# Convolution by half tiles on through the retention, and block 2's output products in another order

## The chip, the cores and the metric
The kernel runs on one core of a Trainium2 chip. The metric is the device time of one execution in microseconds (us); smaller is better. The kernel before took 3770.49 us, the median of three runs (3765.96 to 3771.38). One other execution, the profiled one, took 3763.95 us, of which the trace spans 3762.0.

Engines by the names of the trace: PE multiplies matrices (PEld loads its weights), DVE, ACT and POOL work on elements, SP issues most transfers. A tile has 128 partitions; "128x512" is 128 partitions by 512 elements. PSUM is the memory that PE writes into, in banks of 128x512 f32; SBUF holds everything else on the chip.

## The reference
Three blocks of a network follow one another on 1024 tokens of width 1024. The first is attention, a gated feed-forward layer and a gate. The third is a state-space layer (S5) with a second one behind it. The change is in the second:

```
proj = u @ w_in                       # conv a, b, gate; q, k, v, gate of the retention
a = conv_a * sigmoid(conv_b)
a = causal depthwise conv(a, 31 taps) # each channel by itself, along the tokens
a = silu(layernorm(a))                # over the 1024 channels
y_conv = (a @ conv_pw) * silu(conv_gate)
q, k = rotary(q), rotary(k)
r = retention(q, k, v)                # 4 heads, chunks of 128 tokens, a state from chunk to chunk
y_ret = groupnorm(r) * silu(ret_gate)
y = concat(y_conv, y_ret) @ w_out     # rows 0..1023 of w_out for y_conv, 1024..2047 for y_ret
h = rmsnorm(h + gate * y)
```

## The kernel before, in words
Activations lie with channels on the partitions: 8 tiles of 128 channels x 1024 tokens. A product in full precision (`mm3`, L225 on) splits both operands in a high and a low part (`split`: ACT copies the high part, L159; DVE or POOL subtracts it, L160) and runs three matmuls for each 128 rows and each 512 tokens: high x high (L234), high x low (L235), low x high (L236). One column block of an output is 8 x 3 x 2 = 48 matmuls of 128x512; `weights` loads its 512 KB through a ring of three SBUF tiles called `raw`, which other loads and stores of 128x1024 share.

Block 2 runs in stages. Their order in each engine's queue is fixed when the program is built.
- *Products of w_in with the convolution* (trace 1600 to 2115 us). Products of conv, gate, q, k and v are made by a scheme with seven smaller products (L638 to L640, added up in L650 to L659); 18 groups of 84 matmuls fall into 1690 to 2095. Beside them DVE does the 31 x 8 = 248 taps of the convolution as background jobs (L1149, L1153), each on 128x1024, with the sum in a PSUM tile of two banks. Background jobs stand in a list; products pay into a counter (`rate`, RQ = 6 beside q and k, RT = 8 otherwise), and whenever it holds one, one job is put into the program. What is left is drained before the retention.
- *Retention* (2115 to 2340): 16 steps of 256 tokens (4 heads x 4), each with a mask product (L1369), a state update (L1395, L1397), products out (L1385, L1388), and a normalisation (L1409 to L1415). PE's gaps are filled with the products of the convolution's gate (`fill`). The LayerNorm of the convolution is background work here, RB = 13: sums over channels (POOL, L1268), mean (PE and ACT, L1274, L1275), centring (DVE, L1279), squares (ACT, POOL), scaling (DVE, L1299) and silu. Each head's output is turned (PE, L1426), gated (L1431, L1433) and stored to `yret` (L1435). `X` is then split from the convolution's tiles `A`.
- *Pointwise layer and output products, first half* (2340 to 2546). First `conv_pw` on X (evacuated in L1460 times the gate, split into `G`), then w_out's rows 0 to 1023 on G, evacuated in L1474 onto `hr` (h scaled in the same loop) and stored to `h2`; beside them the loads of `yret` and their split into X, and tables for the S5 block as background work (L1559 and others).
- *block2_out* (2546 to 2640): w_out's rows 1024 to 2047 on X, added to `h2`.

PSUM for products: three banks `mm` and a two-bank tile `acc`, lent anew at some places by `banks()`; two `pa`, two `pb`, one `pc`.

Of the kernel before, what the change touches and what calls it, by code (L numbers as in the profile page):

```python
# [32 lines left out]
RQ = 6  # L33
RT = 8
# [3 lines left out]
RB = 13  # L38
# [19 lines left out]
class Core:  # L58


    def __init__(self, ctx, tc, ins):
# [12 lines left out]

        self.lent = ctx.enter_context(ExitStack())
        self.banks()
# [1056 lines left out]
def block2(core, X, scratch, tabs, keep, after):  # L1133
# [7 lines left out]
    with ExitStack() as st:  # L1141
        cvp = st.enter_context(tc.tile_pool(name="b2_conv", bufs=1, reuse_waits="tile"))
        A = [cvp.tile([P, PAD + S], F32, tag=f"a{c}", name=f"cv_{c}") for c in range(KT)]

        def tap(c, j, state):
# [13 lines left out]
        core.banks("psum_conv")  # L1159
        with tc.tile_pool(name="b2_mix", bufs=1, reuse_waits="tile") as pool:  # L1160
# [37 lines left out]
            def conv(_, c, a, b):  # L1198
# [4 lines left out]
                core.bg += [tap(c, j, state) for j in range(CW)]  # L1203
# [52 lines left out]
            core.paced = None  # L1256
            core.drain()
        scratch["mixed"].close()
        core.banks()
        with tc.tile_pool(name="b2_ret", bufs=1, reuse_waits="tile") as pool:  # L1260
            ln = {}

            def ln_sum(c):
                if c == 0:
                    return
                if c == 1:
                    ln["acc"] = pool.tile([P, S], F32, tag="lnacc", name="ln_acc")
                nc.gpsimd.tensor_tensor(ln["acc"], A[0][:, PAD:] if c == 1 else ln["acc"], A[c][:, PAD:], ALU.add)  # L1268

            def ln_mean():  # L1270
                ln["mu"] = pool.tile([P, S], F32, tag="lnmu", name="ln_mu")
# [5 lines left out]
            def ln_center(c):  # L1277
                a = A[c][:, PAD:]
                nc.vector.tensor_tensor(a, a, ln["mu"], ALU.subtract)  # L1279
                if c == 0:  # L1280
                    ln["var"] = pool.tile([P, S], F32, tag="lnacc", name="ln_var")
                    nc.scalar.activation(ln["var"], a, AF.Square)
                else:
                    sq = core.raw()
                    nc.scalar.activation(sq, a, AF.Square)
                    nc.gpsimd.tensor_tensor(ln["var"], ln["var"], sq, ALU.add)

            def ln_rstd():
                ln["r"] = core.rsqrt(core.token_sums(ln["var"], pool), pool)

            def ln_rows():
                ln["r"] = core.rows(ln["r"], pool)

            def ln_spread():
                ln["rb"] = core.over_partitions(ln["r"], pool, tag="lnmu")
# [10 lines left out]
            def ln_ready(c):  # L1306
                ln_sum(c)

# [3 lines left out]
            core.bg += pause * 4 + [ln_mean] + pause * 4 + [lambda c=c: ln_center(c) for c in range(KT)]  # L1312
            core.bg += pause * 8 + [ln_rstd] + pause * 2 + [ln_rows] + pause * 2 + [ln_spread] + [lambda c=c: ln_scale(c) for c in range(KT)]
# [7 lines left out]
            def conv_gates():  # L1321
                nxt = core.weights(w_in, 0, KT, 2 * D)
                for c in range(KT):
                    w = nxt
                    for half in range(2):
                        ps = core.psum("mm")
                        for k in range(KT):
# [1293 lines left out]
```

## Time and profile before

| | before |
|---|---|
| median of three runs | 3770.49 us (3765.96 to 3771.38) |
| profiled execution / its span | 3763.95 us / 3762.0 us |
| granted clock of PE, mean | 0.957 |
| PE busy | 3450.0 us, 92% of the span |
| DVE busy | 2562.5 us, 68% |
| POOL busy | 1801.3 us, 48% |
| ACT busy | 1568.7 us, 42% |
| chain that ended last: PE / DVE / POOL / DMA | 58% / 13% / 11% / 8% |

Busy shares are means over the whole span; a stage may have another limit, so the rows below are cut by stage. [...] A wait "A <- B" is idle time of A's engine that ended when B was done.

### The profile page before, as it was taken

To read this page: it belongs to the slowest core of one execution; us is meant where nothing else is said; L and a number is where in the kernel's file an instruction comes from. 1 tells how busy PE (TensorE), PEld (TensorE's weight loads), DVE (VectorE), ACT (ScalarE), POOL (GpSimd) and SP (SyncE) were. 2 spreads that over 40 slices of the span, in tenths; PEclk is the share of its full clock that TensorE was granted. 3 is DMA by queue.
4 is the path that set the end of the run, shared out by engine and by line. 5 is a ranking of instruction groups with operands and counts; after the bars stand their busy time and mean duration, and the time that the engine had idled before them with its cause. 6 is when DMAs were issued, how large, how long until landed. Compare 5 with 4: busy or idle time off the path is not lost.

```text
span 3762.0 us, 45800 instructions
## 1 busy us (share of the span) xinstructions
PE 3450.0 (92%) x16540; PEld 2777.5 (74%) x16540; DVE 2562.5 (68%) x3211; ACT 1568.7 (42%) x2729; POOL 1801.3 (48%) x1690
## 2 busy tenths in 40 slices
PE   8999999899998999798889999899899689799998
PEld 7878777777776778576667778678677478577776
DVE  7888897777767556768989665874566366655644
ACT  5666674433334444532223343125443124753334
POOL 2343343456554534477777542427338873331122
PEclk9999999999999999899989999999899899799999
DMA  4111026333325323322212444465443134325513
GB/s 142 37 32 35 28 71 233 107 96 107 107 93 185 112 76 122 113 68 79 79 56 89 139 151 128 116 215 175 135 142 101 52 109 127 96 84 188 176 47 110
DMA packets 431134, 409.84 MB, mean 109 GB/s; under 512 B 34060, under 2 KB 364348, under 8 KB 430908
## 3 DMA queue, kind: packets, MB, share of 16 engines
q1 hardware_dynamic: 396164, 330.27, 28.6%
q0 software_dynamic: 21088, 68.19, 5.0%
q10 hardware_dynamic: 13655, 8.46, 0.8%
q8 instruction: 131, 2.15, 0.2%
q14 instruction: 96, 0.78, 0.1%
HBM read 284.80 MB, written 122.03 MB: 108 GB/s over the span
## 4 chain that ended last, share of the span: by engine, by line
PE 58%; DVE 13%; POOL 11%; DMA 8%; issue 6%; ACT 4%; SPq 0%; ACTq 0%; POOLq 0%; DVEq 0%
PE mm L234 9%; PE mm L236 9%; PE mm L235 9%; PE pb L640 4%; PE pb L638 4%; PE pb L639 4%; DVE wlo L160 3%; PE pa L638 3%; PE pa L640 3%; PE pa L639 3%; POOL sc L1863 2%; POOL s_H L1865 2%; POOL s_H L1864 2%; POOL wlo L160 2%; ACT whi L159 1%
## 5 line engine op out<-in xcount | busy, mean ns | idle before, releaser
L159 ACT ACTIVATE whi<-raw 128x512 fp32r<-128x512 f32 (+3 forms) x610 | 430.9, 736 | 791.2 <-PE pb L639 216.8
L160 DVE TENSOR_TENSOR wlo<-raw,whi 128x512 fp32r<-128x512 f32 (+3 forms) x456 | 551.2, 1231 | 218.4 <-ACT whi L159 214.8
L234 PE MATMUL mm<-x,whi 128*128 128x512 f32 x1152 | 463.1, 403 | 9.3 <-ACT whi L159 4.4
L236 PE MATMUL mm<-x,wlo 128*128 128x512 f32 x1152 | 458.7, 399 | 6.0 <-DVE wlo L160 6.0
L235 PE MATMUL mm<-x,whi 128*128 128x512 f32 x1152 | 461.6, 401 | 0.5 <-DVE x L163 0.3
L493 POOL TENSOR_TENSOR s<-s,f 128x127 f32<-128x127 f32 (+1 forms) x192 | 193.8, 1017 | 294.1 <-DVE f L492 187.5
L1153 DVE SCALAR_TENSOR_TENSOR acc<-cv,par,acc 128x1024 f32<-128x1024 f32 x232 | 298.1, 1285 | 4.3
L638 PE MATMUL pa<-x,whi 128*128 128x512 f32 x648 | 261.5, 404 | 22.5 <-ACT u L659 15.1
L234 PE MATMUL mm<-yc,whi 128*128 128x512 f32 (+1 forms) x656 | 267.4, 408 | 9.2 <-ACT whi L159 5.8
L235 PE MATMUL mm<-yc,whi 128*128 128x512 f32 (+1 forms) x656 | 265.6, 405 | 6.0 <-DVE yc L160 5.9
L640 PE MATMUL pa<-x,wlo 128*128 128x512 f32 x648 | 260.0, 402 | 11.3 <-DVE wlo L160 11.1
L639 PE MATMUL pa<-x,whi 128*128 128x512 f32 x648 | 259.4, 400 | 7.5 <-DVE x L160 7.5
L236 PE MATMUL mm<-yc,wlo 128*128 128x512 f32 (+1 forms) x656 | 263.7, 403 | 1.7 <-DVE wlo L160 1.5
L640 PE MATMUL pb<-x,wlo 128*128 128x512 f32 x576 | 233.3, 410 | 31.2 <-POOL wlo L160 22.5
L234 PEld LDWEIGHTS mm<-x,whi 128*128 128x128 f32 x1152 | 220.2, 191 | 56.2 <-ACT whi L159 4.9
L638 PE MATMUL pb<-x,whi 128*128 128x512 f32 x576 | 236.6, 411 | 26.3 <-ACT whi L159 8.8
L236 PEld LDWEIGHTS mm<-x,wlo 128*128 128x128 f32 x1152 | 219.7, 191 | 52.6 <-DVE wlo L160 7.1
L160 POOL TENSOR_TENSOR wlo<-raw,whi 128x512 fp32r<-128x512 f32 x154 | 215.9, 1421 | 80.6 <-ACT whi L159 80.5
L235 PEld LDWEIGHTS mm<-x,whi 128*128 128x128 f32 x1152 | 220.2, 191 | 45.6 <-DVE x L163 0.6
L639 PE MATMUL pb<-x,whi 128*128 128x512 f32 x576 | 233.2, 405 | 3.1 <-DVE x L160 3.1
L492 DVE TENSOR_TENSOR_SCAN f<-f 128x128 f32<-128x128 f32 (+1 forms) x192 | 195.8, 1034 | 39.5 <-ACT f L485 38.3
L607 POOL TENSOR_TENSOR raw<-raw 128x512 f32<-128x512 f32 x58 | 80.0, 1379 | 246.8 <-DMA raw<-in_ffn_w_in_dram 120.9
(600 smaller groups left out, 8437.0 us busy)
## 6 DMA issues: line engine op xcount, KB each, us to landing
raw<-in_w_in_dram SPq DMA_DIRECT2D x96, 512.0 KB
raw<-in_ffn_w_in_dram SPq DMA_DIRECT2D x44, 512.0 KB
raw<-in_w_out_dram SPq DMA_DIRECT2D x32, 512.0 KB
g<-g_dram SPq DMA_DIRECT2D x56, 256.0 KB
raw<-in_sb_w_in_dram SPq DMA_DIRECT2D x24, 512.0 KB
raw<-in_ada_w_dram SPq DMA_DIRECT2D x24, 512.0 KB
raw<-h_dram SPq DMA_DIRECT2D x18, 512.0 KB
g_dram<-t POOLq DMA_DIRECT2D x8, 1024.0 KB, 4.7
```

Of the source, the lines that this page charges most:

```text
L159: nc.scalar.activation(hi, src, AF.Copy)
L160: return (eng or nc.vector).tensor_tensor(lo, src, hi.bitcast(F32), ALU.subtract).ins
L234: nc.tensor.matmul(ps, w_h, x[:, 0, sl], start=start and k == 0, stop=False)
L235: nc.tensor.matmul(ps, w_h, x[:, 1, sl], start=False, stop=False)
L236: self.last = nc.tensor.matmul(ps, w_l, x[:, 0, sl], start=False, stop=stop and k == n - 1).ins
L492: nc.vector.tensor_tensor_scan(rev, rev, rev, 1.0, ALU.mult, ALU.bypass)
L493: nc.gpsimd.tensor_tensor(s[:, :m - 1], s[:, :m - 1], f[:, 1:m], ALU.mult)
L607: self.eng.tensor_tensor(at["s1"], at["a21"], at["a22"], ALU.add)
L638: nc.tensor.matmul(ps, hi[:, i], x[i][:, 0], start=first and i == 0, stop=False, skip_group_check=more)
L639: nc.tensor.matmul(ps, hi[:, i], x[i][:, 1], start=False, stop=False, skip_group_check=more)
L640: self.core.last = nc.tensor.matmul(ps, lo[:, i], x[i][:, 0], start=False, stop=i == self.N - 1, skip_group_check=more).ins
L1153: nc.vector.scalar_tensor_tensor(out, A[c][:, j:j + S], core.vec("conv_w_2", j * KT + c), state["acc"], ALU.mult, ALU.add)
```

## The change
- The convolution's taps are on half tiles, 128x512, 496 of them, second half of the tokens first; their sum lies in one PSUM bank, `cv`. They are no longer drained before the retention but run on through it.
- PSUM for products: `mm` has two banks in the whole program (three before); `cv` one.
- The LayerNorm's sums and mean stay behind the taps; its centring, variance, scaling and a new split of the convolution into its own tiles `conv` run beside the output products, RY = 7. The S5 tables follow as the last of these jobs, at RS = 2.5 from the last two column blocks on.
- After the retention, `yret` is loaded and split into X, then w_out's rows 1024 to 2047 run first, evacuated onto hr and stored to `h2`. Then the pointwise layer runs on `conv` and is split into X. block2_out does w_out's rows 0 to 1023.
- RQ 9 (6), RT 11 (8), RB 15 (13). The last column of the convolution's gate takes its two halves by turns.

```diff
@@ -30,12 +30,14 @@
 
 
 SB = 6
-RQ = 6
-RT = 8
+RQ = 9
+RT = 11
+RY = 7
+RS = 2.5
 NS = 2
 VA = 0
 VB = 4
-RB = 13
+RB = 15
 PC = 1
 ZR = 10
 YM = 5
-    def banks(self, name="psum_mm"):
-
-        self.lent.close()
-        self.psm = self.lent.enter_context(self.tc.tile_pool(name=name, bufs=1, space=PSUM))
-
     def psum(self, tag, shape=(P, HALF)):
-        pool, bufs = {"mm": (self.psm, 3), "acc": (self.psm, 1), "pa": (self.ps, 2), "pb": (self.ps, 2), "pc": (self.ps, 1)}[tag]
-        return pool.tile(list(shape), F32, tag=tag, name=self.nm(tag), bufs=bufs)
+        bufs = {"mm": 2, "cv": 1, "pa": 2, "pb": 2, "pc": 1}[tag]
+        return self.ps.tile(list(shape), F32, tag=tag, name=self.nm(tag), bufs=bufs)
...
+                at = PAD - CW + 1 + j + half * HALF
                 if j == 0:
-                    state["acc"] = core.psum("acc", (P, S))
-                    nc.vector.tensor_scalar(state["acc"], A[c][:, :S], core.vec("conv_w_2", c),
+                    state["acc"] = core.psum("cv")
+                    nc.vector.tensor_scalar(state["acc"], A[c][:, at:at + HALF], core.vec("conv_w_2", c),
                                             core.vec("conv_b_2", c), ALU.mult, ALU.add)
                     return
-                out = A[c][:, PAD:] if j == CW - 1 else state["acc"]
-                nc.vector.scalar_tensor_tensor(out, A[c][:, j:j + S], core.vec("conv_w_2", j * KT + c), state["acc"],
-                                               ALU.mult, ALU.add)
+                out = A[c][:, PAD + half * HALF:PAD + (half + 1) * HALF] if j == CW - 1 else state["acc"]
+                nc.vector.scalar_tensor_tensor(out, A[c][:, at:at + HALF], core.vec("conv_w_2", j * KT + c),
+                                               state["acc"], ALU.mult, ALU.add)
             return run
-        core.banks("psum_conv")
...
-                core.bg += [tap(c, j, state) for j in range(CW)]
+
+                core.bg += [tap(c, j, half, state) for half in (1, 0) for j in range(CW)]
                 core.bg += [lambda: ready.append(c)]
...
-            core.paced = None
-            core.drain()
...
+            def ln_split(c):
+                if c == KT - 1:
+                    lns.close()
+                pool = parts.enter_context(tc.tile_pool(name=f"b2_c{c}", bufs=1, side="right", reuse_waits="tile"))
+                t = conv[c] = pool.tile([P, 2, S], R32, tag="c", name=f"cv_x{c}")
+                core.split(t[:, 0], t[:, 1], A[c][:, PAD:])
+                cvs[c].close()
+
+            def tables():
+                tabs["pool"] = parts.enter_context(tc.tile_pool(name="s5_tab", bufs=1, side="right", reuse_waits="tile"))
+                core.bg += s5_tables(core, tabs)
+
...
-            core.bg += pause * 4 + [ln_mean] + pause * 4 + [lambda c=c: ln_center(c) for c in range(KT)]
-            core.bg += pause * 8 + [ln_rstd] + pause * 2 + [ln_rows] + pause * 2 + [ln_spread] + [lambda c=c: ln_scale(c) for c in range(KT)]
+            core.bg += pause * 2 + [ln_mean]
+            lnjobs += [lambda c=c: ln_center(c) for c in range(KT)]
+            lnjobs += pause * 2 + [ln_rstd] + pause * 2 + [ln_rows] + pause * 2 + [ln_spread]
+            lnjobs += [lambda c=c: ln_scale(c) for c in range(KT)] + [lambda c=c: ln_split(c) for c in range(KT)[::-1]]
+            lnjobs += [tables]
...
-        for half in range(2):
-            for c in range(KT):
-                core.split(X[c][:, 0, hs(half)], X[c][:, 1, hs(half)], A[c][:, PAD + half * HALF:PAD + (half + 1) * HALF])
+        parts = st.enter_context(ExitStack())
+        rp = parts.enter_context(tc.tile_pool(name="b2_r1", bufs=1, side="right", reuse_waits="tile"))
+        wts = core.weights(w_out, D, KT, 0)
+        for c in range(KT):
+            raw = core.raw()
+            nc.sync.dma_start(raw, yret[c])
+            core.split(X[c][:, 0, :], X[c][:, 1, :], raw)
+        r1b = core.over_partitions(core.rows(scratch["r1"], rp), rp, tag="r1b")
+        core.bg += lnjobs
+        core.rate = RY
+        for m in range(KT):
+            if m:
+                wts = core.weights(w_out, D, KT, m * P)
+            if m == KT - 2:
+                core.rate = RS
+            hr = core.raw()
+            nc.sync.dma_start(hr, scratch["h"][m])
+            nc.vector.scalar_tensor_tensor(hr, hr, core.vec("final_norm", m), r1b, ALU.mult, ALU.mult)
+            ps = [core.psum("mm") for half in range(2)]
+            if m == 0:
+                for k in range(KT):
+                    for half in range(2):
+                        core.mm3(ps[half], wts, X[k:k + 1], half, k0=k, start=k == 0, stop=k == KT - 1)
+            for half in range(2):
+                if m:
+                    core.mm3(ps[half], wts, X, half)
+                nc.vector.scalar_tensor_tensor(hr[:, hs(half)], ps[half], core.mod[:, 2 * KT + m:2 * KT + m + 1],
+                                               hr[:, hs(half)], ALU.mult, ALU.add)
+            nc.gpsimd.dma_start(scratch["h2"][m], hr)
+        for m in range(KT):
+            wts = core.weights(w_pw, 0, KT, m * P)
+            sg = core.raw()
+            nc.sync.dma_start(sg, sgate[m])
+            for half in range(2):
+                ps = core.psum("mm")
+                core.mm3(ps, wts, [conv[c] for c in range(KT)], half)
+                nc.vector.tensor_tensor(sg[:, hs(half)], ps, sg[:, hs(half)], ALU.mult)
+                core.split(X[m][:, 0, hs(half)], X[m][:, 1, hs(half)], sg[:, hs(half)])
+        core.drain()
+        core.rate = 0
...
-            core.bg += s5_tables(core, tabs)
-            core.rate = 1.5
-            for m in range(KT):
...
-            wts = core.weights(w_out, D, KT, m * P)
+            wts = core.weights(w_out, 0, KT, m * P)
```

On DVE, at the end of the retention: `rtk` is the retention's output being normalised, `rs` its reciprocal deviation, `raw` of L1460 a gated pointwise result. Before:

```order
L1410 BN_AGGR mv_3141_18315<-bs_3142_18316 128x2
L1410 BN_AGGR mv_3141_18315<-bs_3143_18319 128x2
L1412 TENSOR_SCALAR rs_3144_18322<-mv_3141_18315 128x2
L1415 TENSOR_SCALAR rtk_3140_18307<-rtk_3140_18307,mv_3141_18315,rs_3144_18322 128x256 x2
L1460 TENSOR_TENSOR raw_3169_18572<-mm_3170_18574,raw_3169_18572 128x512
L1460 TENSOR_TENSOR raw_3169_18572<-mm_3175_18615,raw_3169_18572 128x512
L271 CAST rrow_3157_18468<-b2_r1_12895 128x8
L1684 MEMSET s5_pw_18779 128x32
```

and after (here L1150 is a tap, L154 a split of a loaded yret tile, L1273 a centring):

```order
L1421 TENSOR_SCALAR rs_3136_18470<-mv_3133_18463 128x2
L1150 SCALAR_TENSOR_TENSOR cv_3131_18448<-cv_7_13237,par_79,cv_3131_18448 128x512 x3
L1424 TENSOR_SCALAR rtk_3132_18453<-rtk_3132_18453,mv_3133_18463,rs_3136_18470 128x256 x2
L1150 SCALAR_TENSOR_TENSOR cv_3131_18448<-cv_7_13237,par_79,cv_3131_18448 128x512 x12
L154 TENSOR_TENSOR x_6_6583<-raw_3157_18633,x_6_6583 128x1024
L1150 SCALAR_TENSOR_TENSOR cv_3131_18448<-cv_7_13237,par_79,cv_3131_18448 128x512
L154 TENSOR_TENSOR x_7_6584<-raw_3158_18637,x_7_6584 128x1024
L1150 SCALAR_TENSOR_TENSOR cv_3131_18448<-cv_7_13237,par_79,cv_3131_18448 128x512 x11
L1150 SCALAR_TENSOR_TENSOR cv_7_13237<-cv_7_13237,par_79,cv_3131_18448 128x512
L1273 TENSOR_TENSOR cv_0_13209<-cv_0_13209,ln_mu_16959 128x1024
L1273 TENSOR_TENSOR cv_1_13213<-cv_1_13213,ln_mu_16959 128x1024
```

Of the convolution 25 half taps of the last channel and the splits of `x_6` and `x_7` stand behind the last normalisation (the shown row of L1150 x3 is ahead of it), and seven more centrings follow the rows shown before the first L1467 (scaling of h) and L1476 (evacuation of an output product); before, evacuations of the pointwise layer and first S5 tables stood there.

On PE, at the same place: L1426 (after: L1435) turns the last head's output, `pb` its bank. Before:

```order
L234 MATMUL mm_3175_18615<-x_3_6583,whi_3167_18568 128x512
L235 MATMUL mm_3175_18615<-x_3_6583,whi_3167_18568 128x512
L236 MATMUL mm_3175_18615<-x_3_6583,wlo_3168_18569 128x512
L1426 MATMUL pb_3148_18347<-ident_74,rtk_3140_18307 128x128
L234 MATMUL mm_3175_18615<-x_4_6584,whi_3167_18568 128x512
L1426 MATMUL pb_3148_18347<-ident_74,rtk_3140_18307 128x128 x3
L235 MATMUL mm_3175_18615<-x_4_6584,whi_3167_18568 128x512
L236 MATMUL mm_3175_18615<-x_4_6584,wlo_3168_18569 128x512
L234 MATMUL mm_3175_18615<-x_5_6585,whi_3167_18568 128x512
```

and after (L228 to L230 are the matmuls of a product, L1268 the mean of the LayerNorm, L277 a row spread over the partitions; `mm_3164` and `mm_3165` are the two halves of the first column block, `mm_3176` of the second):

```order
L228 MATMUL mm_3165_18669<-x_7_6584,whi_3149_18605 128x512
L229 MATMUL mm_3164_18668<-x_7_6584,whi_3149_18605 128x512
L230 MATMUL mm_3164_18668<-x_7_6584,wlo_3150_18606 128x512
L229 MATMUL mm_3165_18669<-x_7_6584,whi_3149_18605 128x512
L230 MATMUL mm_3165_18669<-x_7_6584,wlo_3150_18606 128x512
L1268 MATMUL pc_3146_18593<-ln_acc_16958,onesm_16960 128x512
L1268 MATMUL pc_3147_18596<-ln_acc_16958,onesm_16960 128x512
L277 MATMUL pc_3161_18645<-ident_71,rrow_3159_18641 128x128 x8
L277 MATMUL pc_3162_18655<-ident_71,rrow_3159_18641 128x128 x8
L228 MATMUL mm_3176_18756<-x_0_6577,whi_3173_18749 128x512
```

Before, the turning stands within a pointwise product. After, the turning (just ahead of these rows) is followed by the 12 matmuls of `x_6` and `x_7`, the last two of the eight row blocks of the first column block, of which the shown ones are the end; the other six stood between the retention's steps. Then come the mean and the spread rows, and then the second column block.

On SP, the loads there (`yret` tiles, `h`, weights of w_out); before, `yret` loads came one or two with each column block:

```order
L1362 DMA gate_3101_18307<-gate_dram_107 128x2x256
L1455 DMA raw_3157_18633<-yret_dram_92 128x1024
L1455 DMA raw_3158_18637<-yret_dram_92 128x1024
L1466 DMA raw_3163_18665<-h_dram_90 128x1024
L210 DMA raw_3172_18747<-in_w_out_2_dram 128x8x128
L1466 DMA raw_3175_18753<-h_dram_90 128x1024
L210 DMA raw_3183_18829<-in_w_out_2_dram 128x8x128
```

The load of `raw_3172`, the second column block's weights, now stands behind the loads of all eight `yret` tiles; its staging tile is the one that the first block's `h2` store empties.

## Rows read from the trace of the kernel before

**Rows 1.** Windows by stage: start:end, us, busy time (instructions) of PE, PEld, DVE, ACT, POOL, clock, DMA share, GB/s.
```profile
1651.00:1690.00 39.00, 39.00 (x171) 31.89 (x170) 37.70 (x34) 13.38 (x23) 30.62 (x23) 1.00 0.19 54
1690.00:2095.00 405.00, 357.79 (x1468) 279.83 (x1467) 363.75 (x323) 117.23 (x207) 300.09 (x216) 0.94 0.24 75
2115.00:2210.00 95.00, 84.58 (x408) 69.87 (x406) 56.01 (x82) 32.61 (x48) 56.23 (x43) 0.93 0.53 167
2210.00:2340.00 130.00, 130.00 (x672) 111.94 (x672) 65.63 (x142) 55.95 (x86) 41.41 (x54) 1.00 0.44 135
2340.00:2546.00 206.00, 180.67 (x1018) 143.34 (x1017) 155.23 (x283) 42.30 (x58) 72.01 (x31) 0.94 0.57 171
2343.00:2353.00 10.00, 8.67 (x50) 7.12 (x48) 3.98 (x9) 3.68 (x6) 0.00 (x0) 0.99 0.53 136
2353.00:2366.00 13.00, 6.98 (x17) 5.04 (x17) 12.24 (x85) 1.06 (x1) 0.00 (x0) 0.50 0.29 89
```

**Rows 2.** PE's waits, 1690 to 2095: us in total, times, longest.
```profile
PE pb L640 <- POOL wlo L160: 27.4, 16, 5.0
PE pa L638 <- ACT u L659: 12.9, 5, 5.6
```

**Rows 3.** Instructions by form, DVE, 1690 to 2095: count, busy, mean ns, idle before.
```profile
L1153 DVE SCALAR_TENSOR_TENSOR acc<-cv,par,acc 128x1024 f32<-128x1024 f32 x194 | 249.2, 1285 | 3.5
```

**Rows 4.** PE's waits, 2115 to 2340.
```profile
PE pc L1388 <- DVE rstate L1395: 5.5, 1, 5.5
```

**Rows 5.** Timeline of DVE: start, us, instruction; two steps' mask products.
```profile
2145.83 0.41 DVE L1369 TENSOR_TENSOR sm<-pa,rmask 128x256 f32<-128x256 f32 x1
2151.50 0.41 DVE L1369 TENSOR_TENSOR sm<-pa,rmask 128x256 f32<-128x256 f32 x1
```

**Rows 6.** Instructions by form, 2115 to 2340.
```profile
L1279 DVE TENSOR_TENSOR cv<-cv,ln_mu 128x1024 f32<-128x1024 f32 x8 | 16.7, 2159 | 0.3 <-ACT ln_mu L1275 0.3
L1397 DVE SCALAR_TENSOR_TENSOR rstate<-rstate,pa 128x512 f32<-128x512 f32 x24 | 16.3, 679 | 17.3 <-PE pa L1392 15.8 <-PE pc L1388 1.3
L1268 POOL TENSOR_TENSOR ln_acc<-ln_acc,cv 128x1024 f32<-128x1024 f32 x6 | 12.0, 2003 | 0.3
L1299 DVE TENSOR_TENSOR cv<-cv,lnmu 128x1024 f32<-128x1024 f32 x8 | 9.2, 1220 | 0.9 <-ACT lnmu L291 0.9
L1274 PE MATMUL pc<-ln_acc,onesm 128*128 128x512 f32 x4 | 2.1, 608 | 0.0
L1275 ACT ACTIVATE ln_mu<-pc 128x512 f32<-128x512 f32 x2 | 1.2, 597 | 2.8 <-PE pc L1274 2.8
```

**Rows 7.** Timeline, end of the retention, ACT and POOL.
```profile
2335.78 1.02 ACT L1431 ACTIVATE ry<-pb,par 128x256 f32<-128x256 f32 x2 [7.74 <-PE pb L1426]
2336.88 1.29 POOL L1433 TENSOR_TENSOR ry<-ry,gate 128x512 f32<-128x512 f32 x1 [6.82 <-ACT ry L1431]
2338.46 1.14 POOL L1435 DMA_DIRECT2D yret_dram<-ry  x2 [0.30 <-POOL ry L1433]
```

**Rows 8.** DMA issues of the whole span: count, KB each, median us to landing.
```profile
yret_dram<-ry POOLq DMA_DIRECT2D x32, 128.0 KB, 3.4
```

**Rows 9.** Chain of waits, 2410 to 2475: start, us, what.
```profile
2414.32 3.75 DMA raw<-in_w_out_dram
...
2418.18 1.07 ACT whi L159
...
2419.27 1.30 DVE wlo L160
...
2425.10 4.43 DMA raw<-yret_dram
...
2458.76 7.08 DMA h_dram<-raw
```

**Rows 10.** Output products 2340 to 2546: evacuation by form; then PE's longest wait.
```profile
L1474 DVE SCALAR_TENSOR_TENSOR raw<-mm,mod,raw 128x512 f32<-128x512 f32 x16 | 11.9, 745 | 9.3 <-PE mm L236 9.1
PE mm L236 <- DVE wlo L160: 7.5, 2, 6.0
```

More of the change, by code (lines that the diff above doesn't have):

```diff
@@ L1141, in block2, with tap @@
     with ExitStack() as st:
[L1142 to L1145 removed]
+        cvs = [st.enter_context(ExitStack()) for c in range(KT)]
+        A = [cvs[c].enter_context(tc.tile_pool(name=f"b2_conv{c}", bufs=1, reuse_waits="tile")).tile(
+            [P, PAD + S], F32, tag="a", name=f"cv_{c}") for c in range(KT)]
+        def tap(c, j, half, state):
             def run():
+                at = PAD - CW + 1 + j + half * HALF
                 if j == 0:
[L1148 to L1149 removed]
+                    state["acc"] = core.psum("cv")
+                    nc.vector.tensor_scalar(state["acc"], A[c][:, at:at + HALF], core.vec("conv_w_2", c),
                                             core.vec("conv_b_2", c), ALU.mult, ALU.add)
                     return
[L1152 to L1154 removed]
+                out = A[c][:, PAD + half * HALF:PAD + (half + 1) * HALF] if j == CW - 1 else state["acc"]
+                nc.vector.scalar_tensor_tensor(out, A[c][:, at:at + HALF], core.vec("conv_w_2", j * KT + c),
+                                               state["acc"], ALU.mult, ALU.add)
             return run
@@ L1255, in block2 @@
                 turns.pop(0)()
-            core.paced = None
-            core.drain()
         scratch["mixed"].close()
-        core.banks()
+        lns = st.enter_context(ExitStack())
+        lnp = lns.enter_context(tc.tile_pool(name="b2_ln", bufs=1, reuse_waits="tile"))
+        lnjobs, conv = [], {}
         with tc.tile_pool(name="b2_ret", bufs=1, reuse_waits="tile") as pool:
-            ln = {}
+            ln = {"acc": lnp.tile([P, S], F32, tag="acc", name="ln_acc"), "mu": lnp.tile([P, S], F32, tag="mu", name="ln_mu")}
             def ln_sum(c):
@@ L1280, in ln_center @@
                 if c == 0:
[L1281 to L1282 removed]
+                    nc.scalar.activation(ln["acc"], a, AF.Square)
                 else:
@@ L1323, in conv_gates @@
                 for c in range(KT):
-                    w = nxt
-                    for half in range(2):
-                        ps = core.psum("mm")
-                        for k in range(KT):
-                            core.mm3(ps, w, X[k:k + 1], half, k0=k, start=k == 0, stop=k == KT - 1)
-                            if k == KT - 1:
-                                t = pool.tile([P, HALF], F32, tag="t", name=core.nm("cg"), bufs=2)
-                                nc.scalar.activation(t, ps, AF.Silu)
-                                nc.gpsimd.dma_start(sgate[c][:, hs(half)], t)
-                            if half == 1 and k == 0 and c + 1 < KT:
-                                nxt = core.weights(w_in, 0, KT, 2 * D + (c + 1) * P)
-                            yield
+                    w, ps = nxt, {}
+                    order = [(half, k) for half in range(2) for k in range(KT)]
+                    if c == KT - 1:
+                        order = [(half, k) for k in range(KT) for half in range(2)]
+                    for n, (half, k) in enumerate(order):
+                        if k == 0:
+                            ps[half] = core.psum("mm")
+                        core.mm3(ps[half], w, X[k:k + 1], half, k0=k, start=k == 0, stop=k == KT - 1)
+                        if k == KT - 1:
+                            t = pool.tile([P, HALF], F32, tag="t", name=core.nm("cg"), bufs=2)
+                            nc.scalar.activation(t, ps[half], AF.Silu)
+                            nc.gpsimd.dma_start(sgate[c][:, hs(half)], t)
+                        if n == KT and c + 1 < KT:
+                            nxt = core.weights(w_in, 0, KT, 2 * D + (c + 1) * P)
+                        yield
             gates = conv_gates()
@@ L1350, in load @@
                     ts = slice(c2 * 256, (c2 + 1) * 256)
-                    t = [pool.tile([P, 2, 256], F32, tag=f"r{n}", name=core.nm(n), bufs=3) for n in ("q", "k", "v", "gate")]
+                    t = [pool.tile([P, 2, 256], F32, tag=f"r{n}", name=core.nm(n), bufs=3)
+                         for n in ("q", "k", "v", "gate")]
                     for n, y in zip(("q", "k", "gate"), (t[0], t[1], t[3])):
```

45 lines of the change are left out of this document (4 added, 41 removed).

## The prediction
> **What bounds the kernel now.** I read the windows by stage first, then PE's waits in each stage, then the instructions of DVE and POOL there, and last the timeline and the chain of waits around the retention's end. The change touches four stages of block 2, and the reader is to see in [rows 1] where PE has air in each. In the 405 us from 1690 to 2095 the rotary, gate and convolution products run in 18 groups, 22.5 us each; PE works 357.8 us, DVE 363.8. The stretch before it, 1651 to 1690, has the same products with PE never idle: 171 matmuls in 39.0 us, so a group of 84 takes 19.2 us. The 18 groups thus lose 18 x 3.3 = 59 us: 47.2 idle, and 12.2 that their matmuls take longer. From 2115 to 2210 the retention leaves PE idle 10.4 us, from 2210 to 2340 not at all: pointwise products stand between its steps. From 2340 to 2546, the output products beside the S5 tables, PE is idle 25.3 of 206. So there is little to win behind 2115, and everything that the change moves there from under PE's work has to find new cover.
>
> **The products with the convolution.** Today all 248 taps of 128x1024 run before the retention; 206 of them lie in the 18 groups, 194 of one form by [rows 3] and 12 first and last ones: at 1.285 us 265, so 14.7 a group of DVE's 20.2. After, the convolution is 496 taps of 128x512, of which by the order 372 stand before the retention, 99 between its steps and 25 behind the last. The half tap is not in the trace. Its nearest row is the same operation on 128x512, from PSUM too, 679 ns [rows 6], against 1285 for the whole tap: two halves cost 1.36 against 1.29, and the whole change 496 x 0.679 - 248 x 1.285 = 18 us more of DVE. Per group 17.7 half taps are left (the ratio of the new pace, 11 for 8, in halves, by the order), 12.0 us, so DVE falls from 20.2 to 17.5 a group, under PE's 19.2. What does PE wait for there? 27.4 of 47.2 us for the second half of the weights from POOL, which waits for their load, and 12.9 for ACT's copy of a product [rows 2]. The first needs no DVE and need not go. I take back the 12.2 + 19.8 us that are not that wait, and a quarter of the wait since DVE frees the staging tiles earlier: -38; bounds 0 and -59.
>
> [...]
>
> **The retention's start and its bare end.** The centring of the convolution (eight of L1279, 16.7 us of DVE [rows 6]) leaves the retention. It held PE once, 5.5 us, behind the state's update [rows 4]: -6. At the retention's end pointwise products stood between the steps (first fence of PE, before); after, the output products need yret, which the retention itself writes, so by the order the last four steps have only 12 products of 512 columns between them. A step without fill took 5.7 us, from one mask product to the next [rows 5], where DVE had no taps. Now DVE has 5 to 7 half taps in each (3.4 to 4.8 us), and its rows stand in order, so a step waits for them: 9.1 to 10.5 us. Four steps are 14 to 19 us longer, less 3 for the 12 products (0.23 us each, 19.2 / 84): +13; bounds 5, where half the taps fit into the step's own pauses, and 20.
>
> **The transition, on which the sign rests.** Time 0 is the end of DVE's last normalisation. Before, PE is inside pointwise products at that moment and goes on. After, PE can do only the last two tiles' products for column block 0, and must then wait for block 1, as the second fence of PE shows. I follow the chain:
> - The retained rows go out and come back: four transposes (some 0.4), ACT's 1.02, POOL's product 1.29, the store's issue 1.14 [rows 7] and 3.4 to landing [rows 8]: 7.3. The load of a yret tile took 4.43, the halves of a split 1.07 on ACT and 1.30 on DVE [rows 9]: x_6 at 14.1, x_7 two later at 16.1.
> - DVE meanwhile does 12 half taps, then the two splits, then 12 more (8.2): the convolution ends at 24.3. One ln_sum on POOL (2.00) follows: 26.3. Two mean matmuls (0.61 each, up to double at the slow clock) and two ACT copies (0.60 each) [rows 6] give 29.7.
> - Then DVE has eight centrings in a row ahead of the residual's product of block 0. They took 2.16 us each beside POOL's additions; the scalings of the same shape, with POOL idle, 1.22 [rows 6]. I take 2.1, since POOL adds the squares here too: 46.5 (39.5 by the other).
> - The scaling of h (1.3, as the 128x1024 split) and two evacuations of 0.745 [rows 10]: 49.3. The store of this tile, half a us to issue and 3.4 to land: 53.2. Once it landed in 7.08 [rows 9].
> - By the SP fence the weights of block 1 are loaded into the staging tile that this store frees: 3.75 [rows 9], ACT's first half 1.07, DVE's second 1.1 to 3.5 behind the next scaling: 58.4 to 62.
>
> In these some 59 us PE has 12 products of column block 0, the mean's and the rows' spreading, 7.6 us by 0.23 and 0.61 for one at full clock with the slow clock's doubling. So PE loses 51 to 54 us, and I take 51; bounds 40 (the centrings at 1.22, loads overlapped) and 62 (7.08 for the store).
> [...]
> [...]
>
> **The output products.** By the order the S5 tables come in with column block 5 and the pointwise layer, as before they came with pointwise. PE's 25.3 us of idle [rows 1] are 7.5 for two weight splits on DVE [rows 10] and smaller ones; part of them went with the clock of 0.50. The split of X in 16 pieces at the retention's end and the yret loads between products are gone or moved into the transition: I take -10. Against it, PSUM for products is two banks now and was three: DVE's bursts (12.24 us of 13 busy in 2353 to 2366) stall PE as soon as both banks wait for evacuation. Bounds -20 and +10.
> **Two banks elsewhere.** Attention's and block 3's products lose the third bank too. Nothing in these traces prices it: below nothing is excluded for it, since a bank less starts nothing earlier. +4, bounds 0 and 10.
>
> **Sum.** -38 - 6 + 13 + 51 + 4 - 10 + 4 = +18 us. Against the profiled execution, 3763.95 us: 3782. The median of the runs is 6.5 above that execution, so 3788.
>
> **Rivals.**
> - *Faster, the mix pays for all.* The 18 groups run at the 19.2 of 1651 to 1690 (-59), the tables' air goes (-20), and the transition is 40: -59 - 6 + 5 + 40 - 20 + 4 = -36, 3735 us. For it: that stretch has DVE 37.7 of 39.0 us busy and no stall [rows 1], so a full DVE alone doesn't hold PE. Against: the weights' wait of 27.4 us. It decides where the transition is under the gain of the mix.
> - *The two cancel.* A mix of -45 and a transition of 45 with the rest as above: about 0, 3771. For it: both ends are well within bounds.
> - *Slower still, two banks.* In the pointwise part four to eight table bursts of DVE stop PE 4 us each on top: +16 to +32, 3812. For it: DVE's 155 of 206 us there, and 12.24 of 13 in one stretch.
> - *The mix gains nothing*, as its wait is POOL's weights: 3820. It is the upper end.
>
> **How the numbers follow.** The forecast and its neighbours 0.44; faster 0.22; cancel 0.18; two banks 0.12; no gain in the mix 0.04. About 0.2% (7.5 us) is what a measurement of this kernel can tell from no change. Of the 0.18, 0.02 are put on the faster side: faster 0.24, within 0.2% 0.16, slower 0.60 (0.44 + 0.12 + 0.04). The likeliest's own range is 3772 to 3806; the range at 8 in 10 reaches to 3738 on one side, and to 3822 on the other.
>
> **What would show it.** The mix: 18 groups of about 20.4 us and half taps of 0.68. The retention: last steps of 9 to 10 us, with half taps on DVE between a step's rows. The transition: PE nearly bare for 50 us between the last transposes and the first product of column block 1, granted clock 0.50 behind it, eight centrings in one row on DVE, and the store of h2 then the load of w_out ending last. Products of pointwise: the wait for evacuations no larger than before. I am wrong where PE's gap is under 30 us, or where the groups stay at 22.5 or fall to 19.2.

## The result and the profile after

The changed kernel took 3801.34 us (median of 4 runs, 3796.82 to 3803.18): 1.0091 times the time of before, 95% interval 1.0074 to 1.0107, so 34 us slower. The ratio is to the kernel before as it ran beside the changed one (median 3768.22 us of four runs). The profiled execution took 3801.98 us.

Where the time went I read by counting PE's work: both kernels run 16540 matmuls, and the k-th starts earlier or later in the trace after. The order differs, so the k-th is a count of work done and not always the same matmul.

| k-th matmul | stage there | after minus before, us |
|---|---|---|
| 7600 | products of w_in | -3.0 |
| 8800 | end of their groups | -11.4 |
| 10025 | last steps of the retention | -12.4 |
| 10150 | output products | +47.7 |
| 11200 | block2_out | +32.7 |
| 12000 | block 3 | +33.7 |
| 16000 | near the end | +44.5 |
| 16539 | last | +38.0 |

So 3 us were gained up to the 7600th, the products gave 8, the retention 1, its end cost 60, the output products gave 15 back, and block 3 swings between -2 and +12 and ends at +5.

Windows of the kernel after (columns as in [rows 1], whose stages they answer to):

```profile
1651.00:1690.00 39.00, 38.99 (x170) 31.53 (x169) 36.51 (x49) 13.05 (x23) 30.31 (x24) 1.00 0.19 55
1690.00:2085.00 395.00, 350.73 (x1451) 276.10 (x1450) 327.83 (x406) 115.01 (x203) 294.27 (x216) 0.95 0.25 77
2110.00:2140.00 30.00, 26.01 (x121) 20.61 (x119) 19.52 (x19) 6.08 (x9) 12.13 (x8) 1.00 0.64 208
2140.00:2215.00 75.00, 75.00 (x385) 64.63 (x384) 52.70 (x104) 21.69 (x36) 21.68 (x30) 1.00 0.51 156
2275.00:2310.00 35.00, 27.51 (x149) 22.81 (x147) 34.16 (x73) 12.66 (x21) 15.59 (x20) 0.96 0.36 121
2310.00:2369.00 59.00, 14.12 (x37) 8.37 (x36) 41.24 (x38) 14.70 (x17) 23.61 (x12) 0.53 0.17 58
2390.00:2579.00 189.00, 174.98 (x1009) 138.07 (x1008) 160.09 (x291) 51.54 (x68) 71.11 (x30) 0.98 0.53 151
```

In the groups DVE fell from 90% to 83% of the stretch, and PE is idle as much as before: 44.3 of 395 us, 47.2 of 405 in [rows 1]. From 2310 to 2369 it works 14 of 59 us.

PE's waits after, first in 1690 to 2085, then in 2300 to 2420:

```profile
PE pb L634 <- POOL wlo L154: 35.3, 17, 4.8
PE pa L632 <- ACT u L653: 5.0, 2, 3.7
```
```profile
PE mm L228 <- ACT whi L153: 23.8, 1, 23.8
PE mm L228 <- ACT x L153: 9.5, 1, 9.5
PE pc L1268 <- POOL ln_acc L1263: 9.3, 1, 9.3
PE pb L1435 <- DVE rtk L1424: 5.8, 1, 5.8
```

The first block answers to [rows 2]: the wait for POOL's weights grew from 27.4 to 35.3 us while DVE had less to do. The second block is the transition: yret (9.5), the sum of the channels behind the taps (9.3), the last turning behind the normalisation (5.8), and the weights of block 1 (23.8). DVE's timeline there shows what they stand behind:

```profile
2309.19 0.73 DVE L1424 TENSOR_SCALAR rtk<-rtk,mv,rs 128x256 f32<-128x256 f32 x2
2309.83 9.46 DVE L1150 SCALAR_TENSOR_TENSOR cv<-cv,par,cv 128x512 f32<-128x512 f32 x12
2320.31 1.22 DVE L154 TENSOR_TENSOR x<-raw,x 128x1024 fp32r<-128x1024 f32 x1 [1.02 <-ACT x L153]
...
2323.24 9.45 DVE L1150 SCALAR_TENSOR_TENSOR cv<-cv,par,cv 128x512 f32<-128x512 f32 x12
2340.32 17.75 DVE L1273 TENSOR_TENSOR cv<-cv,ln_mu 128x1024 f32<-128x1024 f32 x8 [7.63 <-ACT ln_mu L1269]
2357.99 1.27 DVE L1467 SCALAR_TENSOR_TENSOR raw<-raw,par,r1b 128x1024 f32<-128x1024 f32 x1
2359.37 1.41 DVE L1476 SCALAR_TENSOR_TENSOR raw<-mm,mod,raw 128x512 f32<-128x512 f32 x2
```

Half taps, splits, half taps, eight centrings, scaling, two evacuations: the queue of the order's rows, with nothing between them but the two waits shown.

The eight centrings are of two kinds, which a mean of 2.29 us hides. By form, from 2340.2 to 2344.8 and from 2345 to 2357.9, then POOL's timeline beside the second four:

```profile
L1273 DVE TENSOR_TENSOR cv<-cv,ln_mu 128x1024 f32<-128x1024 f32 x4 | 4.6, 1221 | 7.6 <-ACT ln_mu L1269 7.6
```
```profile
L1273 DVE TENSOR_TENSOR cv<-cv,ln_mu 128x1024 f32<-128x1024 f32 x4 | 13.2, 3358 | 0.0
```
```profile
2344.21 12.78 POOL L1279 TENSOR_TENSOR ln_acc<-ln_acc,raw 128x1024 f32<-128x1024 f32 x4 [9.44 <-ACT raw L1278]
```

Until POOL begins to add squares, a centring takes 1.22 us; from then on one centring and one addition are done every 3.28 us.

The half tap itself, from the profile's page (mean ns of one behind the busy time):

```profile
L1150 DVE SCALAR_TENSOR_TENSOR cv<-cv,par,cv 128x512 f32<-128x512 f32 x480 | 360.7, 751 | 10.2
```

Twelve in a row take 9.46 us, one every 0.79. Four whole taps in a row, in the timeline of before, one every 1.32 ((5.25 - 1.285) / 3):

```profile
2100.42 5.25 DVE L1153 SCALAR_TENSOR_TENSOR acc<-cv,par,acc 128x1024 f32<-128x1024 f32 x4
```

So the convolution costs DVE 496 x 0.79 - 248 x 1.32 = 65 us more.

### The profile page after: what moved, and what is told of

It reads as the page before. It is cut to its first block, busy times and chain, and to the rows that moved or that the text cites. A ratio compares the mean times of both kernels' runs of the same rounds, so it can differ in the third digit from the quotient of the medians.

```text
span 3800.1 us, 46065 instructions
## 1 busy us (share of the span) xinstructions
PE 3450.0 (91%) x16540; PEld 2773.8 (73%) x16540; DVE 2598.0 (68%) x3451; ACT 1570.8 (41%) x2723; POOL 1816.5 (48%) x1690
## 5 line engine op out<-in xcount | busy, mean ns | idle before, releaser
L154 DVE TENSOR_TENSOR wlo<-raw,whi 128x512 fp32r<-128x512 f32 (+3 forms) x456 | 536.4, 1199 | 207.6 <-ACT whi L153 203.4
L228 PE MATMUL mm<-x,whi 128*128 128x512 f32 x1152 | 462.7, 402 | 46.8 <-ACT whi L153 23.8
L230 PE MATMUL mm<-x,wlo 128*128 128x512 f32 x1152 | 459.1, 399 | 2.9 <-DVE wlo L154 2.9
L1150 DVE SCALAR_TENSOR_TENSOR cv<-cv,par,cv 128x512 f32<-128x512 f32 x480 | 360.7, 751 | 10.2
L487 POOL TENSOR_TENSOR s<-s,f 128x127 f32<-128x127 f32 (+1 forms) x192 | 211.9, 1115 | 290.9 <-DVE f L486 143.0
L228 PEld LDWEIGHTS mm<-x,whi 128*128 128x128 f32 x1152 | 219.4, 191 | 95.7 <-ACT whi L153 23.9
L230 PEld LDWEIGHTS mm<-x,wlo 128*128 128x128 f32 x1152 | 219.3, 190 | 50.3 <-DVE wlo L154 5.1
L154 POOL TENSOR_TENSOR wlo<-raw,whi 128x512 fp32r<-128x512 f32 x154 | 219.4, 1445 | 65.5 <-ACT whi L153 65.4
L228 PE MATMUL mm<-yc,whi 128*128 128x512 f32 (+1 forms) x528 | 216.3, 410 | 14.5 <-DVE xc L2085 7.4
L229 PE MATMUL mm<-yc,whi 128*128 128x512 f32 (+1 forms) x528 | 215.2, 408 | 0.1
L230 PE MATMUL mm<-yc,wlo 128*128 128x512 f32 (+1 forms) x528 | 214.3, 407 | 0.0
```

What stands on the lines that cost most here:

```text
L154: return (eng or nc.vector).tensor_tensor(lo, src, hi.bitcast(F32), ALU.subtract).ins
L228: nc.tensor.matmul(ps, w_h, x[:, 0, sl], start=start and k == 0, stop=False)
L229: nc.tensor.matmul(ps, w_h, x[:, 1, sl], start=False, stop=False)
L230: self.last = nc.tensor.matmul(ps, w_l, x[:, 0, sl], start=False, stop=stop and k == n - 1).ins
L487: nc.gpsimd.tensor_tensor(s[:, :m - 1], s[:, :m - 1], f[:, 1:m], ALU.mult)
L1150: nc.vector.scalar_tensor_tensor(out, A[c][:, at:at + HALF], core.vec("conv_w_2", j * KT + c), state["acc"], ALU.mult, ALU.add)
```

## The experiments

Times are medians; the ratio is to the kernel before, run on the same chip (median 3766.82 us beside experiments 1 to 4, 3763.49 beside 5 to 8, 3762.93 beside 9 to 12). "After" is the changed kernel.

**1. Without the taps' work.** 464 of 496 half taps are left out.
```diff
-core.bg += [tap(c, j, half, state) for half in (1, 0) for j in range(CW)]
+core.bg += [tap(c, j, half, state) if j in (0, CW - 1) else (lambda: None) for half in (1, 0) for j in range(CW)]
```


> The changed kernel without 29 of the 31 taps of every channel half: first and last tap stay, 464 of 496 half taps are left out. What ends PE's idle time in the products of w_in? Theory (weights): the second half of the weights from POOL ends it, DVE does not, so 1690 to 2085 us keeps its length within 10 us, with the wait for POOL's wlo still above 25 us. Rival (DVE): half taps cost 0.751 us in the trace after, so DVE held the groups; they then run at 19.2 to 20 us, 35 to 50 us less. Behind it both expect the same: without taps the last retention steps are 2 to 4 us shorter each (-10) and PE's gap at the retention's end is about 31 us and not 59, since the mean is ready at once and only the eight centrings (17.8) and the store and load of the staging tile are left. Total 3755 by the theory, 3715 by the rival.

3760.13 us, ratio 0.9984 (0.9973 to 0.9995). The window of the groups and PE's longest wait in it:
```profile
1690.00:2085.00 395.00, 353.13 (x1445) 277.91 (x1444) 138.07 (x133) 115.17 (x203) 295.35 (x214) 0.94 0.25 78
```
```profile
PE pb L634 <- POOL wlo L154: 28.3, 13, 4.4
```
DVE is busy 138 us of 395, and PE gets through 1445 matmuls where it did 1451 with all taps. DVE does not hold the groups; my theory stands, the forecast's term falls. From the 7600th to the 8800th matmul this kernel gains 4.5 us on before, where after gained 8.4 with all its taps. Most of the 41 us saved lie at the retention's end (at the 10150th matmul 35 us ahead of after).

**2. A fourth tile for weights there.**
```diff
-raw = core.raw()
+raw = self.stage() if which and self.stage else core.raw()
```


> The changed kernel with one more SBUF tile for the second weight load of each group in the products of w_in, so that its load need not wait for one of the three raw tiles. Theory (weights): the groups' wait for POOL's wlo (35.3 us in the trace after) falls below 20, and the kernel is 15 to 30 us faster, 3770 to 3786. Rival (DVE, or POOL's own work): the load comes earlier, but the wait turns into one for POOL or DVE, and the time stays within 5 us of 3801.

3797.89 us, 1.0083 (1.0063 to 1.0102). The wait for POOL's weights fell from 35.3 to 24.0 us, and the time by less than its spread: the rival is nearer. Staging is not what sets the pace.

**3. Weights of block 1 ahead.**
```diff
+w1 = core.weights(w_out, D, KT, P)
 r1b = core.over_partitions(core.rows(scratch["r1"], rp), rp, tag="r1b")
...
-                wts = core.weights(w_out, D, KT, m * P)
+                wts = w1 if m == 1 else core.weights(w_out, D, KT, m * P)
```


> The changed kernel with the weights of the second column block loaded ahead of the scaling of h, so that they don't wait for the store of h2. Theory: the last link of the chain at the retention's end goes and PE waits for a product bank instead, which the first evacuation behind the eight centrings gives back at 50 us after the last normalisation and not at 59: 8 us faster, 3793. Rival (loads or something ahead of the centrings end the gap): no change, 3801 within 3. If the banks don't matter, PE starts the block right behind the mean at 34 and 25 us are gained, 3776.

3797.39 us, 1.0080 (1.0060 to 1.0100). As said, the wait for weights turned into one for a product bank:
```profile
PE mm L228 <- DVE raw L1477: 17.9, 2, 15.0
```
The 10075th matmul comes 8 us earlier than after; of that, 4 us show in the medians, within their spread.

**4. Blocks 0 and 1 ahead of the centrings.** As 3, one block ahead throughout; seven pauses ahead of the centrings; and, moved ahead of the yret loads:
```diff
-r1b = core.over_partitions(core.rows(scratch["r1"], rp), rp, tag="r1b")
+r1b = core.over_partitions(core.rows(scratch["r1"], rp), rp, tag="r1b", psum="pa")
```


> The changed kernel with the centrings moved behind: each column block's weights are loaded one block ahead, the row that scales h is spread ahead of the output products in another PSUM bank, and seven empty background jobs stand before the first centring. The order then has the evacuations of blocks 0 and 1 and the weights of block 2 ahead of the eight centrings. Theory (the centrings in DVE's queue, then store and load, make the gap): PE begins block 1 at about 25 us after the last normalisation instead of 59, does blocks 1 and 2 and then waits some 12 us for the centrings: 20 to 25 us faster, 3777 to 3781. Rival (the trip of yret through DRAM and the 25 left half taps make most of it): under 10 us, above 3791.

3789.41 us, 1.0060 (1.0040 to 1.0079): 12 us won, between the two. Block 1 began early, and then the centrings cost in one wait about what they had cost before:
```profile
PE mm L228 <- DVE raw L1477: 28.2, 3, 23.6
```

**5. Experiment 1 with the weights split on DVE.**
```diff
-mix.on_pool = Mixed.ORDER
+mix.on_pool = ()
```


> As the first experiment (464 of 496 half taps left out), and the second half of the weights in the products of w_in is subtracted on DVE, which is idle there two thirds of the time, and not on POOL. Theory (POOL's place in the weights' way ends the groups' waits: its adds and splits are one queue of 17 us a group): PE idles under 20 us in 1690 to 2085, groups fall to 20 us, and the kernel is 25 to 45 us faster than the first experiment, 3715 to 3735. Rival (three raw tiles and their loads set the pace, whoever splits): idle stays at 40 us, 3755 within 5.

3749.39 us, 0.9956 (0.9941 to 0.9971): 11 us under experiment 1, not 25 to 45. The groups' window, and PE's longest waits from 1690 to 2100:
```profile
1690.00:2085.00 395.00, 366.34 (x1531) 291.18 (x1531) 219.89 (x268) 122.98 (x218) 152.66 (x103) 0.95 0.27 81
```
```profile
PE pa L632 <- ACT u L653: 14.2, 6, 3.2
PE pb L634 <- DVE wlo L154: 8.5, 4, 2.9
```
1531 matmuls in place of 1445: with DVE nearly free, POOL's split holds a part of the groups. The waits that are left are for ACT's copies and for the split on DVE.

**6. Centrings paced behind evacuations**, on 4: `pause * 15` ahead, one pause behind each, RY 9, and
```diff
-nc.vector.scalar_tensor_tensor(hr[:, hs(half)], ps[half], ...
+core.paced = nc.vector.scalar_tensor_tensor(hr[:, hs(half)], ps[half], ...
```


> The fourth experiment with the centrings spread out: two or four at a time behind evacuations of the output products (fifteen empty jobs ahead, one between two centrings, and every job queued behind the last evacuation; RY 9). Theory (in the fourth experiment PE lost 23.6 us waiting for an evacuation behind eight centrings): 10 to 18 us faster than the fourth, 3771 to 3779. Rival (what the centrings don't hold up here, the scalings and splits of the LayerNorm hold up later before the pointwise layer): within 5 of 3789.

3793.18 us, 1.0072 (1.0055 to 1.0089). No gain on 4: the rival. One wait of 23.6 became four, 19.2 in all.

**7. Experiment 6 with `RB = 20`.**

> The sixth with RB 20 for 15: all half taps then stand before the retention's last normalisation and none behind. Theory: evacuations of blocks 0 and 1 come as soon as yret is back; PE's idle time behind the last normalisation falls to the trip of yret (10 us) and a few us; 8 to 15 us faster than the sixth, 3758 to 3770, so about the time of before. Rival (the taps then make the steps of the retention longer by what they free at its end, 25 taps x 0.75 = 19 us): no faster than the sixth.

3785.86 us, 1.0055 (1.0039 to 1.0071): 7 us under 6, so short of 8 to 15. At the 11200th matmul it is 3 us behind before, at the 12000th 13, at the end 20. Why it stays 20 us above experiment 12, which has the same RB without the other edits, is open; the traces say where: 17 us ahead of 12 at the 10150th matmul, 4 behind at the 12000th, 17 behind at the end, so 22 are lost on the way to block 3 and 13 in it. Against 6 the same RB gained 18 us up to the 12000th, of which block 3 left 10 in the trace.

**8. The kernel before with half taps alone** (RQ 12, RT 16, drained as there; the diff of the change's `tap`).

> The kernel before with its convolution by half tiles alone, all drained before the retention as there (RQ 12, RT 16 half taps, so the same work beside each product; order and other banks of before). By the trace after a half tap takes 0.751 us, so DVE's 363.8 us in the 18 groups become 408 of 405. Theory: DVE is now as full as the groups are long, and the products stretch: 10 to 40 us slower than before, 3777 to 3807. Rival (weights alone set the groups, DVE has slack even so): within 5 us of 3767.

3832.03 us, 1.0167 (1.0141 to 1.0194): worse than both ends. At the 8800th matmul it is level with before, at the 9600th 67 us behind: DVE's 65 us more, by the count above, pile up in the list, and the drain ahead of the retention pays for them. Its windows, end of the groups and the drain's beginning:
```profile
1690.00:2085.00 395.00, 349.01 (x1432) 274.98 (x1431) 356.53 (x447) 112.92 (x200) 295.54 (x215) 0.94 0.23 73
2085.00:2150.00 65.00, 45.70 (x201) 36.51 (x200) 60.88 (x81) 21.54 (x32) 34.75 (x22) 0.87 0.43 138
```

**9. The order alone**: the changed kernel with whole taps, drained, and `banks()` of before (RQ 6, RT 8).

> The changed kernel with the convolution of the kernel before: whole taps of 128x1024 in two banks, drained ahead of the retention, three product banks (RQ 6, RT 8); of the change the order of the output products and the LayerNorm's place stay. By its order no tap and no centring stands behind the last normalisation. Theory (half taps spilled to the retention's end make most of the loss; the order itself costs only the trip of yret and the store and load of the staging tile, some 30 us for block 1 in place of 59, less 16 won among the output products): 0 to 12 us slower than before, 3765 to 3778. Rival (the order alone makes the loss): 3790 and more.

3766.45 us, 1.0008 (0.9997 to 1.0018): no change. The new order costs nothing in sum, but not because the transition is free: from the 10025th to the 10150th matmul it loses 27 us, with PE waits of 12.9 for block 1's weights and 10.4 for yret. It was 8 us ahead at the 10025th, of which 6 came in the retention, now without its centrings, and the output products give 13 back.

**10. Experiment 9 with 6's edits** (RB stays at 15, where 7 has 20).

> The ninth with the seventh's edits (weights one block ahead, row that scales h in another bank, centrings paced behind evacuations, RY 9). Theory: block 1 no longer waits for the store of h2, so PE's idle time behind the last normalisation is the trip of yret, about 10 us: 8 to 12 us faster than the ninth, 3755 to 3768, so at or under the time of before. Rival (DVE's work in this stage sets its length, as in the sixth): within 4 of the ninth.

3766.00 us, 1.0010 (1.0001 to 1.0019). Block 1 begins 17 us earlier than in 9 (10075th matmul), and all of it is gone by the 12000th: the rival.

**11. The kernel before with two product banks.**
```diff
-"mm": (self.psm, 3)
+"mm": (self.psm, 2)
```


> The kernel before with two product banks in place of three, nothing else. Theory (a bank less costs nothing: each half block takes PE 5.5 us, an evacuation 0.75): within 5 us of 3767. Rival (attention, the tables' bursts of DVE and block 3 make PE wait for evacuations): 10 us slower and more.

3751.78 us, 0.9967 (0.9954 to 0.9980): 11 us faster than before, the other way than either theory. It beats both kernels. 9 us of it come between the 10400th and the 10800th matmul, beside the tables:
```profile
2340.00:2537.00 197.00, 179.98 (x1017) 142.88 (x1016) 155.38 (x279) 42.25 (x57) 73.72 (x32) 0.95 0.58 178
```
PE is idle 17 us there and was 25.3 [rows 1]. The order of PE's rows differs in 5111 of 16540 places; which of them does it stays open. Not all of it is a gain: from the 12000th to the 13000th matmul this kernel and the nine others with two product banks (after, 1 to 7, 12) lose 7 us on before, and from the 16000th to the 16200th they win 7 back; 8, 9 and 10, with three banks, do neither.

**12. The changed kernel with one number.**
```diff
-RB = 15
+RB = 20
```


> The changed kernel with RB 20 for 15 alone: the 25 half taps then stand before the last normalisation, the eight centrings right behind it, ahead of the splits of x_6 and x_7. Theory (the chain taps, mean, centrings, scaling of h, store, load): PE begins block 1 about 31 us after the last normalisation and not 59, the last steps of the retention take some 8 us more: 15 to 20 us faster than the changed kernel, 3781 to 3786. Rival (the trip of yret bounds it, taps lie beside it): within 5 of 3801.

3766.35 us, 1.0008 (0.9998 to 1.0019): the loss is gone to within the interval, 35 us where I expected 15 to 20. DVE at the retention's end:
```profile
2309.68 2.41 DVE L1424 TENSOR_SCALAR rtk<-rtk,mv,rs 128x256 f32<-128x256 f32 x2
2318.18 9.17 DVE L1273 TENSOR_TENSOR cv<-cv,ln_mu 128x1024 f32<-128x1024 f32 x8 [6.09 <-ACT ln_mu L1269]
2327.27 2.35 DVE L154 TENSOR_TENSOR x<-raw,x 128x1024 fp32r<-128x1024 f32 x2
2329.54 1.28 DVE L1467 SCALAR_TENSOR_TENSOR raw<-raw,par,r1b 128x1024 f32<-128x1024 f32 x1
2332.36 1.60 DVE L1476 SCALAR_TENSOR_TENSOR raw<-mm,mod,raw 128x512 f32<-128x512 f32 x2 [1.54 <-PE mm L230]
2345.49 1.23 DVE L154 TENSOR_TENSOR wlo<-raw,whi 128x1024 fp32r<-128x1024 f32 x1 [11.52 <-ACT whi L153]
```
Block 1 starts at 2345.5, some 33 us behind the last normalisation and not 59: the chain, as expected. The centrings themselves are done 15 us behind the last normalisation and not 48. Of these 33 us, 24 come ahead of them, from the 25 taps (19 us), which found room in the retention (the 10025th matmul comes 1 us later than after, not 8), and from two splits that now stand behind; 9 are the centrings' own, 1.22 us each. Behind them the splits, a wait for PE and a longer store and load give 7 back. The centrings by form, 2310 to 2370, after and here:
```profile
L1273 DVE TENSOR_TENSOR cv<-cv,ln_mu 128x1024 f32<-128x1024 f32 x8 | 17.8, 2290 | 7.6 <-ACT ln_mu L1269 7.6
```
```profile
L1273 DVE TENSOR_TENSOR cv<-cv,ln_mu 128x1024 f32<-128x1024 f32 x8 | 9.2, 1220 | 6.1 <-ACT ln_mu L1269 6.1
```
After, POOL adds squares beside the last four centrings; here its first addition comes at 2329.67, when all eight are over. At the 12000th matmul 25 of the 35 us are there; the other 10 lie in block 3 and are not explained. It swings from program to program: from the 14000th to the 15000th matmul experiments 1, 4, 6, 11 and 12 gain 6 to 7 us on before, the others between a gain of 1 and a loss of 3.

## Why the prediction was right

The sign and the place were right, by the chain; the number fell within the range partly by luck. The largest term was 30 us too good, in the trace, and 13 of that were taken back by the retention (8 better than its +7) and the output products (5). From the last normalisation's end at 2309.92, forecast and trace in us:

| | forecast | measured |
|---|---|---|
| x_6 split | 14.1 | 11.6 |
| convolution done | 24.3 | 22.8 |
| sum of channels done | 26.3 | 24.9 |
| mean copied | 29.7 | 30.4 |
| centrings done | 46.5 | 48.1 |
| two evacuations done | 49.3 | 50.9 |
| block 1 begins | 58.4 to 62 | 59.1 |

The end of the retention cost 60 us against 51 + 4. No run shows the 4, a charge for PE's clock behind the gap. The trace after shows a granted clock (a share of full speed) of 0.53 from 2310 to 2369, 0.50 from 2369 to 2375, 0.93 from there to 2380 and 1.00 to 2390; [rows 1] had 0.50 where PE was busy 7 of 13 us. Where nothing else held them, block 1's matmuls of 128x512 began 0.43 us apart up to the twelfth, at 2375.36, and 0.23 apart from 2375.98 on; my estimate from these is 12 x 0.20 = 2.4 us. Two readings in the chain were off. The centrings at 2.1 us stand for a mean: in [rows 6], too, four of the eight took 1.22 us, three 3.36 and one 2.30, by what POOL did beside them; the sum came out near, 17.8 us against 16.8. And block 1's first matmul needs the first half of its weights alone: PE waited for ACT's copy, not for DVE's split, so the forecast's own rows give 58.0.

*The products, -38: the step that failed.* It took back the 12.2 + 19.8 us "that are not that wait" on the belief that DVE held them. 8 us came. Experiment 1 shows the same groups with DVE almost free, and 5 that POOL's split holds part of them. The count of groups was wrong as well: the window 1690 to 2095 holds 1404 matmuls of theirs, 16.7 groups and not 18, so a group took 24.2 us; after, by the same count (1387 in 395 us), 23.9. The groups stayed, which the forecast had named as a sign of being wrong; DVE's share fell to 19.9 us a group, not to 17.5. The rival with no gain in the mix had the mechanism, at a chance of 0.04 and at 3820 us, where its own sum gives 3788 + 38 = 3826; it should have had far more, since [rows 2] named POOL and ACT, and no row named DVE.

*The half tap.* I took 0.679 from the state's update, whose result goes to SBUF; the tap's goes back to PSUM and takes 0.751, and 0.79 from start to start. That the destination makes the difference no run shows. In the groups that cost nothing, in 8 all of it. That taps spill into the retention, and 25 to its end, is fixed by the order and its paces (RQ, RT, RB) and not by the price of a tap; the price makes those 25 take 19 us there and not 17.

*The retention, -6 + 13.* The last steps took 9.6, 8.2 and 9.2 us between mask products, near the forecast; but the earlier steps were better filled, and the sum was -1. With no taps or few in the retention, 9 gains 6.5 us there and 1 gains 4.5, so the -6 came about and the taps cost 4 to 6, not 13.

*Output products, -10:* -15. *Two banks elsewhere, +4:* open. Of the gain of 11 in the kernel before (11), 9 lie among the output products; attention is 1 us ahead there and block 3 gains 2.5. In the change attention is 3 ahead and block 3 loses 5, in a block that swings by 10 without a known cause. No run has the change with three banks.

*Cause and remedy.* Half taps alone lose 66 us by the trace (8), the order alone nothing (9), and both together lose 34, or nothing once the background work of the retention is paced at 20 and not 15 (12). Of the 60 us at the retention's end, 27 come with the order alone (9) or with few taps (1), and the output products and the retention pay for them. Shown by 1 and 12 is that most of the other 33 go once the half taps no longer stand behind the last normalisation. In both runs the centrings also fall to 1.22 us each; that 9 of the 33 are theirs, from standing beside POOL, is read from the rows, and no run changes it alone. The last 10 of the 35 us that 12 wins lie in block 3 and stay open.

## What to carry to other kernels

Before an engine's work is cut, find a wait that names that engine: a busy share of 90% is not one. When work is let run past a stage's end, count what of it stands behind the last instruction that the next stage waits for, and follow that queue to the next product; here a pacing constant moved it and was worth 25 us of the loss at that place, and 35 in the median. Starting a block earlier gains nothing where the same engine's work only waits a block later.

## What the runs showed of the hardware

A DVE subtraction of 128x1024 took 1.22 us with POOL idle and 3.36 while POOL added tiles of the same shape, both in the trace after: from 2344.87 a centring and an addition were done every 3.28 us, where alone the one took 1.22 (from 2340.32) and two additions 4.76 (from 2361.65, DVE idle). The records of the two engines overlap; what makes both longer no run shows. The means of 2.29 there and 2.16 in [rows 6] mix the two kinds. In 12 the last two normalisations took 2.41 us (L1424 above) in place of 0.73 after, beside an addition that POOL had begun just before them:

```profile
2309.62 1.99 POOL L1263 TENSOR_TENSOR ln_acc<-ln_acc,cv 128x1024 f32<-128x1024 f32 x1
```

Halving a tap whose sum stays in PSUM cost 0.79 x 2 (after, twelve from 2309.83) against 1.32 us (before, four from 2100.42) from start to start.

A PSUM bank less for products made the kernel before faster by 0.33% (11), where I had expected nothing or a loss. The program's order changed with it, so this shows nothing of the bank as such.
